# Which queue issues which transfer: 113 loads and stores leave the sync queue of a one-core decoder layer

## The chip, the core and the metric

One core of one Trainium2 chip runs the whole layer in one launch. The metric is device time in microseconds (us), median of three runs. Five engines work side by side, each on its own list of instructions, strictly in the order of that list: TensorE (PE in the profile, its weight loads PEld), VectorE (DVE), ScalarE (ACT), GpSimd (POOL) and SyncE (SP). SP computes nothing; it only issues transfers. A transfer is issued by one engine's list and waits there, at its place, until all it needs is ready; what stands behind it on that list waits too. Transfers that SP and ACT issue run on a hardware queue (q1 in the profile), those that POOL issues on a software queue (q0), and POOL's can also add to what lies in the destination (`accum_op=OP.add`).

## What is computed

```python
proj = x @ w_in[l]                       # 1024 tokens x 2048 -> one wide projection, split in 13
# group A: indexer scores, top-256 causal keys per query, latent attention, SiLU gate
score = einsum('bqh,bqhs->bqs', wb, relu(einsum('bqhd,bsd->bqhs', qib, k_idx)))
_, sel = top_k(where(causal, score, -inf), 256)
logits = einsum('bqhc,bqkc->bhqk', qb, ckv[sel]) * 128 ** -0.5 + rel_bias[t5_bucket(rel)]
o = einsum('bhqk,bqkc->bqhc', softmax(logits), ckv[sel])
y_a = einsum('bthc,hcd->bthd', o, w_uv[l]) * silu(z_a)
# group B: mLSTM, chunkwise, 4 heads, after a causal conv and SiLU on q and k; norm, two gates
y_m = norm(mlstm(q, k, v, i, f)) * sigmoid(o_m) * silu(z_m)
x = layer_norm(ALPHA * x + concat([y_a, y_m]) @ w_out[l])
```

## The kernel before

Every projection is a product of two float32 matrices with each operand split in a high and a low part, three matmuls a block (`xh,wh`, `xl,wh`, `xh,wl`). The blocks of 2 x 2 products are combined in Strassen's manner: seven products instead of eight, with summed weights (`t1` to `t4`) and summed inputs (`s1` to `s4`).

A weight block of 256 KB goes this way: SP loads it into one of six `wraw` buffers; for a sum, POOL adds a second block to it in flight (L722, L823), which has to wait until the first has landed; ACT rounds it to `wh` (L743, L850), DVE takes the rest as `wl` (L744, L851), and twelve matmuls of 512 columns use the pair. There are four buffers each for `wh` and `wl`.

The program runs in these stages (us from the start of the profile): narrow and query projections (0 to 230); 20 units of projections over the first half of the input, with the indexer's scores (240 to 690), each unit's partial result stored as 1 MB in `part_d` (L791); the value projections in two halves (`Values`, 690 to 845), with stores to `v_d` (L892) and loads of new input forms `u` (L284, L288); the second half of the units with the mLSTM of four heads (845 to 1292); attention (1292 to 1500); the output product with partial sums `z_d` (L1527) and the norm (to the end).

In the second half each unit first loads its partial result back (`res<-part_d`, L710), adds four products to it, and what the unit is for is done with it: a conv for q and k, a scaling and a store to `qa_d` (L974, L975), or a SiLU and a store to `gate_a` (L209, L210). Two `res` tiles take turns. Each half of a head loads gate rows broadcast to 128 partitions (`ri`, L994, then a POOL select L995), and its values (`vraw`, L1027), which ACT and DVE split (`vh`, `vl`) ahead of the state's matmuls (`num`, `up`).

The order on each engine is not that of the source: a scheduler simulates the program while it is built and puts each instruction on its engine's list where its simulation finds it ready; `urgent()` and the other priorities decide among those ready. So a change of a queue moves instructions on other engines too.

Of the kernel before, what the change touches and what calls it, by code (L numbers as in the profile page):

```python
# [30 lines left out]
DV = 256  # L31
# [14 lines left out]
G_QA = 16  # L46
# [56 lines left out]
def kernel(ctx, tc, a, out):  # L103
# [101 lines left out]
    def gate_attention(j, ps, z=None):  # L205
        z = s4("z") if z is None else z
        with urgent():
            for p_, s in zip(ps, halves):
                act.activation(z[:, s], p_, AF.Silu)  # L209
        sync.dma_start(gate_a[j], z)  # L210


    mi = [s4("mi", (P, min(3, 8 - 3 * i), NM)) for i in range(3)]
# [27 lines left out]
    for k in range(4):  # L241
        r, ws, xs = {}, [], []
# [227 lines left out]
    with tc.high_priority(offset=I_PRIO), tc.issue_after(marks[n + 46].ins):  # L470
        for j in range(2):
            cn = s4("cn")
            for h in range(2):
                ps = bank("cnt")
                for c in range(4):
                    pe.transpose(ps[:, c * P:(c + 1) * P],
                                 narrow(h * 4 + c, M_C + j * P, M_C + (j + 1) * P), ident)
                vec.tensor_scalar(cn[:, halves[h]], ps, small(S_KVG + j), None, op0=OP.mult)
            sync.dma_start(c_d[j], cn)
        gr = s4("gr", (2 * H_M, T))  # L480
        for h in range(2):
            ps = bank("gnt")
            for c in range(4):
                pe.transpose(ps[0:2 * H_M, c * P:(c + 1) * P], narrow(h * 4 + c, M_IF, NM), ident)
            act.copy(gr[:, halves[h]], ps[0:2 * H_M])
        sync.dma_start(if_d[:], gr)
# [136 lines left out]
    def search():  # L623

        yield from count(None, OP.is_ge)
        vec.tensor_scalar(sgn, cnt, TOPK - 0.5, -1.0, op0=OP.is_lt, op1=OP.mult)
        vec.memset(sel, 0)
        for bit in range(30, -1, -1):
            vec.scalar_tensor_tensor(out=cand, in0=sel, scalar=1 << bit, in1=sgn,  # L629
                                     op0=OP.bitwise_or, op1=OP.bitwise_xor)  # L630
            yield from count_both(cand.bitcast(F32))
            vec.tensor_tensor(take, cnt, bound, op=OP.is_le)
            vec.scalar_tensor_tensor(out=sel, in0=take, scalar=bit, in1=sel,
                                     op0=OP.logical_shift_left, op1=OP.bitwise_or)
        vec.tensor_tensor(thr.bitcast(I32), sel, sgn, op=OP.bitwise_xor)
        yield from count(thr, OP.is_gt)
        vec.tensor_scalar(take, cnt, TOPK - 0.5, None, op0=OP.is_ge)
        vec.tensor_scalar(low, sel, 0xffff, None, op0=OP.bitwise_and)
        vec.tensor_scalar(high, sel, 16, None, op0=OP.logical_shift_right)
        vec.tensor_tensor(low, low, take, op=OP.add)  # L640
        vec.tensor_scalar(take, low, 16, None, op0=OP.logical_shift_right)
        vec.tensor_tensor(high, high, take, op=OP.add)
        vec.tensor_scalar(low, low, 0xffff, None, op0=OP.bitwise_and)
        vec.scalar_tensor_tensor(out=sel, in0=high, scalar=16, in1=low,
                                 op0=OP.logical_shift_left, op1=OP.bitwise_or)
        vec.tensor_tensor(thr.bitcast(I32), sel, sgn, op=OP.bitwise_xor)
        yield from count(thr, OP.is_gt)
        vec.tensor_scalar(need, cnt, -1.0, float(TOPK), op0=OP.mult, op1=OP.add)
        for t in range(2, 8):
            w = (t + 1) * P  # L650
            col = slice(t - 2, t - 1)
            eq = s4("eq", (P, T), BF16)[:, 0:w]
            vec.tensor_scalar(eq, sc[t], thr[:, col], None, op0=OP.is_equal)
            yield
            pre = s4("pre")[:, 0:w]
            vec.tensor_tensor_scan(out=pre, data0=one_col[:, 0, 0:1].broadcast_to([P, w]), data1=eq, initial=0.0,
                                   op0=OP.mult, op1=OP.add)
            yield
            vec.scalar_tensor_tensor(out=pre, in0=pre, scalar=need[:, col], in1=eq,
                                     op0=OP.is_le, op1=OP.mult)  # L660
            yield
            vec.scalar_tensor_tensor(out=pre, in0=sc[t], scalar=thr[:, col], in1=pre,
                                     op0=OP.is_gt, op1=OP.max)
            yield
            m = s4("m", (P, T), BF16)[:, 0:w]
            vec.tensor_scalar(m, pre, -BIG, BIG, op0=OP.mult, op1=OP.add)
            sync.dma_start(mask_d[t][:], m)
            yield

    steps = search()  # L670
# [23 lines left out]
    class Unit:  # L694


        def __init__(self, i, g, second, X):
            self.i, self.g, self.second, self.X = i, g, second, X
            self.raw = {}
            if second and i == NU - 1:  # L700
                self.res = [s4("res") for _ in range(2)]
                with urgent():
                    for n in range(2):
                        sync.dma_start(self.res[n], part_d[i, :, n])
                return
            res = x_tile("res", (P, 2, T), F32)
            self.res = [res[:, n] for n in range(2)]
            if second:
                with urgent():
                    sync.dma_start(res, part_d[i])  # L710
            else:
                self.kept = res

# [73 lines left out]
        def end(self):  # L787
            self.product(self.pa, "t4", "a22", False)
            self.add(self.res[0][:, bot], self.pa, True)
            if not self.second:  # L790
                sync.dma_start(part_d[self.i], self.kept)  # L791

    heads = [[G_HEAD + 6 * h + 2 * j for j in range(3)] for h in range(H_M)]
    others = [G_QA + j for j in (0, 2, 4, 6)] + [G_ZA + j for j in (0, 2, 4, 6)]
# [19 lines left out]
    class Values:  # L814
# [11 lines left out]
        def run(self, second, X):  # L826
# [54 lines left out]
            def add(i, n, ps, first=False, minus=False, last=False):  # L881
                for t in range(4):
# [6 lines left out]
                        else:  # L889
                            act.copy(dst, ps[t])  # L890
                    if last and t % 2:
                        sync.dma_start(v_d[n, i, :, t - 1:t + 1], self.c[i, n][t // 2])  # L892

            pa = [pj() for _ in range(4)]
            block(0, 0)
# [71 lines left out]
    def other(g, r):  # L967

        for i in range(2):
            if g < G_QA:  # L970
                gate_attention(g - G_ZA + i, [r[i][:, s] for s in halves], r[i])
            else:
                with tc.high_priority(offset=I_PRIO):
                    act.mul(r[i], r[i], -DH ** -0.5)  # L974
                sync.dma_start(qa_d[g - G_QA + i], r[i])  # L975

    def y_sign(left, upper):

# [2 lines left out]
    def mlstm_store(h, j, hs, sg):  # L981
        for half in range(2):
            ps = bank("ht")
            for c in range(4):
                pe.transpose(ps[:, c * P:(c + 1) * P], hs[half][:, c, j * P:(j + 1) * P], ident)
            vec.scalar_tensor_tensor(out=sg[:, halves[half]], in0=ps, scalar=y_sign(h < 2, half == 0),
                                     in1=sg[:, halves[half]], op0=OP.mult, op1=OP.mult)
        sync.dma_start(y_d[8 + 2 * h + j], sg)

    def mlstm_half(h, half, n, q, k):  # L990

        s = halves[half]
        ri = s4("ri", (P, 2, 512))
        sync.dma_start(ri, bcast_rows(rows_d[h, :, s]))  # L994
        pool.affine_select(out=ri[:, 0].rearrange("p (c l) -> p c l", l=L),  # L995
                           in_=ri[:, 0].rearrange("p (c l) -> p c l", l=L),
                           compare_op=OP.is_ge, fill=BIG, base=0,
# [26 lines left out]

    def split_values(h, half):
        raw = s4("vraw", (P, 4, DV))
        sync.dma_start(raw, v_d[h // 2, half, :, :, h % 2 * DV:(h % 2 + 1) * DV])  # L1027
        vh, vl = s4("vh", (P, 4, DV + 2), F32R), s4("vl", (P, 4, DV + 2), F32R)
        split(vh[:, :, 0:DV], vl[:, :, 0:DV], raw)
        act.copy(vh[:, :, DV:DV + 2], one_col)  # L1030
# [401 lines left out]
    class Product:  # L1432
# [76 lines left out]
        def add(self, i, n, ps, first=False, minus=False, last=False):  # L1509
# [14 lines left out]
            if last and not self.c:  # L1524
                for t, z in enumerate(self.z[i, n]):
                    r0 = 4 * i + 2 * t
                    sync.dma_start(z_d[r0:r0 + 2, :, n].rearrange("t p c -> p t c"), z)  # L1527

        def run(self, then, following=None):
            pa = [lps() for _ in range(4)]  # L1530
# [143 lines left out]
```

## Time and profile before

| | |
|---|---|
| median of 3 runs | 1829.42 us (1828.87 to 1832.27) |
| the profiled execution | 1828.79 us, of which the span of the trace is 1827.0 us |
| TensorE busy | 1774.0 us, 97% of the span |
| VectorE, ScalarE, GpSimd busy | 1400.2, 943.5, 263.5 us |
| transfers | SP issues 794, GpSimd 192, ScalarE none |

The profiled execution lies within the range of the runs, 0.63 us under their median; 1.79 us of it lie outside the span. An engine's busy time leaves out the issuing of transfers and its waits. In the rows of the timeline the brackets give the engine's idle time ahead of an instruction and what ended it.

### The profile page before, as it was taken

To read this page: it belongs to the slowest core of one execution; us is meant where nothing else is said; L and a number is where in the kernel's file an instruction comes from. 1 tells how busy PE (TensorE), PEld (TensorE's weight loads), DVE (VectorE), ACT (ScalarE), POOL (GpSimd) and SP (SyncE) were. 2 spreads that over 40 slices of the span, in tenths; PEclk is the share of its full clock that TensorE was granted. 3 is DMA by queue.
4 is the path that set the end of the run, shared out by engine and by line. 5 is a ranking of instruction groups with operands and counts; after the bars stand their busy time and mean duration, and the time that the engine had idled before them with its cause. 6 is when DMAs were issued, how large, how long until landed. Compare 5 with 4: busy or idle time off the path is not lost. (4 is left out here: it accounts for less than half of the span.)

```text
span 1827.0 us, 25483 instructions
## 1 busy us (share of the span) xinstructions
PE 1774.0 (97%) x8613; PEld 1493.9 (82%) x8613; DVE 1400.2 (77%) x2674; ACT 943.5 (52%) x1728; POOL 263.5 (14%) x316
## 2 busy tenths in 40 slices
PE   8999999999999999999999999999989999999997
PEld 8788888887878888788888887878788987888885
DVE  8666677777877778887877786877898876676787
ACT  6343266566666658322555564565665654333410
POOL 3101110000100010100101000010454530011000
PEclk9999999999999999999999999999999999999998
DMA  9986254445575657887656656475776447965764
GB/s 329 324 296 196 84 166 120 111 127 136 136 207 143 167 166 240 291 251 199 204 174 180 198 149 181 108 202 176 236 202 159 118 115 216 279 191 123 188 190 139
DMA packets 148732, 338.82 MB, mean 185 GB/s; under 512 B 16104, under 2 KB 25576, under 8 KB 142456
## 3 DMA queue, kind: packets, MB, share of 16 engines
q1 hardware_dynamic: 121880, 280.16, 46.5%
q0 software_dynamic: 26720, 57.03, 16.5%
q8 instruction: 68, 1.11, 0.2%
q14 instruction: 64, 0.52, 0.1%
HBM read 259.40 MB, written 91.35 MB: 192 GB/s over the span
## 5 line engine op out<-in xcount | busy, mean ns | idle before, releaser
L753 PE MATMUL pj<-xh,wh 128*128 128x512 f32 x960 | 376.4, 393 | 5.9 <-DVE res L762 4.3
L753 PE MATMUL pj<-xl,wh 128*128 128x512 f32 x960 | 375.2, 391 | 0.0
L753 PE MATMUL pj<-xh,wl 128*128 128x512 f32 x960 | 371.2, 392 | 1.2 <-DVE wl L744 1.2
L743 ACT CAST wh<-wraw 128x512 fp32r<-128x512 f32 x280 | 172.2, 619 | 207.8 <-PE pj L753 92.3
L744 DVE TENSOR_TENSOR wl<-wraw,wh 128x512 fp32r<-128x512 f32 x280 | 191.3, 687 | 48.9 <-ACT wh L743 43.3
L753 PEld LDWEIGHTS pj<-xh,wh 128*128 128x128 f32 x960 | 180.6, 188 | 45.1 <-ACT pqh L108 3.0
L753 PEld LDWEIGHTS pj<-xh,wl 128*128 128x128 f32 x960 | 180.4, 188 | 38.1 <-DVE wl L744 2.3
L753 PEld LDWEIGHTS pj<-xl,wh 128*128 128x128 f32 x960 | 180.5, 188 | 34.5
L722 POOL DMA_DIRECT2D wraw<-wg x80 | 68.2, 856 | 753.3 <-DMA wraw<-wg 172.8
L762 DVE TENSOR_TENSOR res<-res,pj 128x512 f32<-128x512 f32 x160 | 109.2, 682 | 54.4 <-PE pj L753 44.9
L583 DVE SCALAR_TENSOR_TENSOR sc<-r,wi,sc 128x384 f32<-128x384 f32 (+2 forms) x90 | 84.1, 948 | 30.7 <-ACT r L578 30.0
L578 ACT ACTIVATE r<-sc 128x384 f32<-128x384 f32 (+3 forms) x160 | 79.2, 524 | 51.1 <-PE sc L577 37.3
L108 ACT CAST wh<-wraw 128x512 fp32r<-128x512 f32 (+2 forms) x88 | 50.2, 575 | 80.3 <-PE lps L1486 22.6
L614 ACT ACTIVATE junk<-sc,cand 128x512 bf16<-128x512 f32 (+2 forms) x93 | 86.7, 934 | 6.0 <-DVE cand L629 6.0
L109 DVE TENSOR_TENSOR wl<-wraw,wh 128x512 fp32r<-128x512 f32 (+2 forms) x88 | 56.7, 647 | 31.6 <-ACT wh L108 24.2
L617 DVE TENSOR_SCALAR_CACHE_REDUCE junk<-sc,cand 128x384 bf16<-128x384 f32 (+2 forms) x93 | 80.1, 875 | 0.9
L1318 POOL TENSOR_TENSOR nm<-mask,tb 128x256 f32<-128x256 bf16 (+3 forms) x64 | 66.6, 1119 | 83.5 <-DVE mn L1325 69.4
L753 PE MATMUL pb<-xh,wh 128*128 128x512 f32 x160 | 62.9, 393 | 0.0
L753 PE MATMUL pb<-xh,wl 128*128 128x512 f32 x160 | 62.5, 391 | 0.0
L753 PE MATMUL pb<-xl,wh 128*128 128x512 f32 x160 | 62.4, 390 | 0.0
L1330 ACT ACTIVATE lg<-lg,mn 128x256 f32<-128x256 f32 (+3 forms) x64 | 50.4, 790 | 15.8 <-DVE mn L1325 15.7
L341 PE MATMUL pj<-xh,wh 128*128 128x512 f32 x128 | 51.4, 402 | 4.5 <-ACT wh L108 4.5
(561 smaller groups left out, 4471.6 us busy)
## 6 DMA issues: line engine op xcount, KB each, us to landing
wraw<-wg SPq DMA_DIRECT2D x232, 256.0 KB, 4.1
wraw<-wg POOLq DMA_DIRECT2D x80, 256.0 KB, 5.2
part_d<-res SPq DMA_DIRECT2D x20, 1024.0 KB, 4.9
res<-part_d SPq DMA_DIRECT2D x19, 1024.0 KB, 8.5
wraw<-wo SPq DMA_DIRECT2D x64, 256.0 KB, 4.5
wraw<-wv SPq DMA_DIRECT2D x48, 256.0 KB, 5.9
v_d<-v SPq DMA_DIRECT2D x16, 512.0 KB, 5.3
z<-x SPq DMA_DIRECT2D x16, 512.0 KB, 4.2
```

What stands on the lines that cost most here:

```text
L109: vec.tensor_tensor(lo, src, hi.bitcast(F32), op=OP.subtract)
L341: last_mm[0] = pe.matmul(ps[u], w[:, k], x[:, k], start=start and k == 0 and n == 0, stop=k == 3 and n == 2, skip_group_check=True)
L578: act.activation(r[:, s], ps, AF.Relu)
L583: vec.scalar_tensor_tensor(out=sc[t], in0=r, scalar=wcol, in1=sc[t], op0=OP.mult, op1=OP.add)
L614: act.activation(junk, sc[t], AF.Sign, scale=-1.0, bias=th[:, t - 2:t - 1], accum_out=cnt[:, t - 2:t - 1])
L617: vec.tensor_scalar(junk, sc[t], th[:, t - 2:t - 1], 0.0, op0=OP.is_lt, op1=OP.add, accum_out=cnt[:, t - 2:t - 1])
L722: pool.dma_start(r, a["wg"][self.g + more[1], :, k0:k0 + 4, :], accum_op=OP.add)
L743: last_cast[0] = act.copy(wh, src)
L744: last_low[0] = vec.tensor_tensor(wl, src, wh.bitcast(F32), op=OP.subtract)
L753: last_mm[0] = pe.matmul(ps, w[:, k], x[:, k], start=start and k == 0 and n == 0, stop=k == 3 and n == 2, skip_group_check=True)
L762: vec.tensor_tensor(dst, dst, ps, op=OP.subtract if minus else OP.add)
L1318: last_sum[0] = pool.tensor_tensor(nm[:, 0:ws], mask[t][:, w - ws:w], tb[:, off:off + ws], op=OP.add)
```

## The change

The same transfers are made, in the same sizes, between the same tiles. 113 of SP's 794 are issued by another engine: 36 by ACT (the stores to `part_d`, `qa_d` and `gate_a`), 77 by POOL (2 to `c_d`, 6 to `mask_d`, 16 to `v_d`, 8 of `sg` to `y_d`, 8 to `z_d`; and 21 loads of `res`, 8 of `ri`, 8 of `vraw`). SP keeps the weights and the other loads.

```diff
@@ gate_attention (L210)
-        sync.dma_start(gate_a[j], z)
+        act.dma_start(gate_a[j], z)
@@ L479
-            sync.dma_start(c_d[j], cn)
+            pool.dma_start(c_d[j], cn)
@@ search (L667)
-            sync.dma_start(mask_d[t][:], m)
+            pool.dma_start(mask_d[t][:], m)
@@ Unit.__init__ (L704, L710)
-                        sync.dma_start(self.res[n], part_d[i, :, n])
+                        pool.dma_start(self.res[n], part_d[i, :, n])
...
-                    sync.dma_start(res, part_d[i])
+                    pool.dma_start(res, part_d[i])
@@ Unit.end (L791)
-                sync.dma_start(part_d[self.i], self.kept)
+                act.dma_start(part_d[self.i], self.kept)
@@ Values.run (L892)
-                        sync.dma_start(v_d[n, i, :, t - 1:t + 1], self.c[i, n][t // 2])
+                        pool.dma_start(v_d[n, i, :, t - 1:t + 1], self.c[i, n][t // 2])
@@ other (L975)
-                sync.dma_start(qa_d[g - G_QA + i], r[i])
+                act.dma_start(qa_d[g - G_QA + i], r[i])
@@ mlstm_store (L988)
-        sync.dma_start(y_d[8 + 2 * h + j], sg)
+        pool.dma_start(y_d[8 + 2 * h + j], sg)
@@ mlstm_half (L994)
-        sync.dma_start(ri, bcast_rows(rows_d[h, :, s]))
+        pool.dma_start(ri, bcast_rows(rows_d[h, :, s]))
@@ split_values (L1027)
-        sync.dma_start(raw, v_d[h // 2, half, :, :, h % 2 * DV:(h % 2 + 1) * DV])
+        pool.dma_start(raw, v_d[h // 2, half, :, :, h % 2 * DV:(h % 2 + 1) * DV])
@@ Product.add (L1527)
-                    sync.dma_start(z_d[r0:r0 + 2, :, n].rearrange("t p c -> p t c"), z)
+                    pool.dma_start(z_d[r0:r0 + 2, :, n].rearrange("t p c -> p t c"), z)
```

The engines' lists differ at three places that matter below. The first is on SP, in the value projections, around the loads of two input forms (`u_7111` and `u_7119`). Before:

```order
L821 DMA wraw_7253<-wv 128x512
L284 DMA u_7111<-form_d1s3_82 128x2048
L892 DMA v_d_75<-v_6489 128x1024
L892 DMA v_d_75<-v_6490 128x1024
L288 DMA u_7119<-xT 128x512 x4
```

In the changed kernel, on SP at the same place:

```order
L821 DMA wraw_7253<-wv 128x512
L284 DMA u_7111<-form_d1s3_82 128x2048
L288 DMA u_7119<-xT 128x512 x4
L879 DMA v_7143<-v_d_75 128x1024
```

The two stores between the loads are gone from SP. The second place is the mLSTM's third head, where its first half loads its values (`vraw_10173`). Before, on SP:

```order
L719 DMA wraw_10508<-wg 128x512
L710 DMA res_10279<-part_d_84 128x2048
L1027 DMA vraw_10173<-v_d_75 128x4x256
L719 DMA wraw_10531<-wg 128x512
```

In the changed kernel the same two loads stand on POOL, with a weight block's second part, which POOL adds to `wraw_10508`, between them:

```order
L722 DMA wraw_10451<-wg 128x512
L995 AFFINE_SELECT ri_10142<-ri_10142 128x512
L710 DMA res_10279<-part_d_84 128x2048
L722 DMA wraw_10508<-wg 128x512
L1027 DMA vraw_10173<-v_d_75 128x4x256
```

On ACT the cast of these values (`vh_10175`) stood before behind the weight casts `wh_10302` and `wh_10433`:

```order
L743 CAST wh_10302<-wraw_10202 128x512
L743 CAST wh_10433<-wraw_10431 128x512
L108 CAST vh_10175<-vraw_10173 128x4x256
L1031 ACTIVATE vl_10176<-one_col_68 128x4x2
L743 CAST wh_10454<-wraw_10451 128x512
L743 CAST wh_10474<-wraw_10451 128x512
```

In the changed kernel it stands behind two more weight casts and a sigmoid with its table load:

```order
L743 CAST wh_10433<-wraw_10431 128x512
L743 CAST wh_10454<-wraw_10451 128x512
L961 ACT_TABLE_LOAD
L961 ACTIVATE res_10065<-res_10065 128x1024
L743 CAST wh_10474<-wraw_10451 128x512
L108 CAST vh_10175<-vraw_10173 128x4x256
```

The third place is the fourth head, where POOL's list in the changed kernel puts the gate rows `ri_10983` and the partial result `res_11151` behind a weight block (`wraw_11380`) and two stores; before, SP had them ahead of the load of that same block:

```order
L722 DMA wraw_11323<-wg 128x512
L722 DMA wraw_11380<-wg 128x512
L988 DMA y_d_74<-sg_10321 128x1024
L988 DMA y_d_74<-sg_10570 128x1024
L994 DMA ri_10983<-rows_d_93 128x2x512
L710 DMA res_11151<-part_d_84 128x2048
L995 AFFINE_SELECT ri_10983<-ri_10983 128x512
```

So at this place a load that had the weights' queue to itself for a moment now waits for a weight block.

## Rows read from the trace of the kernel before

**Rows 1.** The page's first part: engine, busy us (share of the span), instructions.

```profile
PE 1774.0 (97%) x8613; PEld 1493.9 (82%) x8613; DVE 1400.2 (77%) x2674; ACT 943.5 (52%) x1728; POOL 263.5 (14%) x316
```

**Rows 2.** Windows: stretch, length, busy us of PE, PEld, DVE, ACT, POOL.

```profile
690.00:845.00 155.00, 150.97 (x661) 123.38 (x660) 135.81 (x233) 66.61 (x112) 12.01 (x14) 1.00 0.84 264
845.00:1292.00 447.00, 438.12 (x2110) 364.67 (x2109) 339.99 (x639) 254.76 (x412) 45.98 (x57) 1.00 0.61 173
...
200.00:250.00 50.00, 49.72 (x238) 40.98 (x238) 34.52 (x68) 22.63 (x54) 6.77 (x10) 1.00 0.42 135
```

**Rows 3.** Waits of the SP queue, whole span: us in total, times, longest.

```profile
SPq L719 <- DVE wraw L740: 279.9, 37, 14.5
...
SPq L479 <- DVE cn L478: 33.2, 1, 33.2
```

**Rows 4.** Waits of PE in the mLSTM's stage, 845 to 1292.

```profile
PE pj L753 <- DVE res L762: 4.3, 4, 2.6
PE num L112 <- ACT vh L108: 3.0, 2, 2.0
```

**Rows 5.** Timeline of SP, 744 to 770: start, us, what.

```profile
746.84 0.33 SPq L284 DMA_DIRECT2D u<-form_d1s  x1
748.62 1.51 SPq L892 DMA_DIRECT2D v_d<-v  x2
750.41 3.64 SPq L288 DMA_DIRECT2D u<-xT  x4
```

**Rows 6.** Timeline of ACT, 752 to 764.

```profile
757.88 1.05 ACT L108 CAST xh<-u 128x1024 fp32r<-128x1024 f32 x1 [3.49 <-DMA u<-xT]
```

**Rows 7.** Timeline of PE, 758 to 764.

```profile
759.99 0.50 PE L861 MATMUL pj<-wh,xh 128*128 128x512 f32 x1 [0.69 <-ACT v L890]
...
762.95 0.49 PE L861 MATMUL pj<-wh,xh 128*128 128x512 f32 x1 [1.75 <-ACT v L890]
```

**Rows 8.** Timeline of SP, 1098 to 1124.

```profile
1111.84 0.54 SPq L1027 DMA_DIRECT2D vraw<-v_d  x1
```

**Rows 9.** Timeline of POOL, 1105 to 1133.

```profile
1117.54 0.86 POOL L722 DMA_DIRECT2D wraw<-wg  x1 [9.38 <-DMA wraw<-wg]
```

**Rows 10.** Timeline of ACT, 1112 to 1123.

```profile
1120.94 1.05 ACT L108 CAST vh<-vraw 128x1024 fp32r<-128x1024 f32 x1 [5.86 <-DMA vraw<-v_d]
```

**Rows 11.** Timeline of PE, 1119 to 1123.

```profile
1122.05 0.39 PE L112 MATMUL num<-vh,pqh 128*128 128x258 f32 x1 [1.96 <-ACT vh L108]
```

**Rows 12.** Windows: the eleventh figure is the granted clock, 1.00 being full.

```profile
1123.50:1126.90 3.40, 3.40 (x13) 3.03 (x14) 3.22 (x6) 1.56 (x2) 0.00 (x0) 0.50 0.00 0
```

**Rows 13.** The tile vraw: issue to landing of its eight loads.

```profile
DMA to landing us min/median/max: 5.1/5.9/8.3
```

**Rows 14.** The chain that ended last, by time: start, us, what.

```profile
1607.64 10.88 PE lps L1486 x48
```

**Rows 15.** Transfer issues from 845 to 1292: KB each, median us to landing.

```profile
res<-part_d SPq DMA_DIRECT2D x17, 1024.0 KB, 8.5
```

**Rows 16.** Timeline of SP, 1198 to 1230.

```profile
1201.65 0.33 SPq L710 DMA_DIRECT2D res<-part_d  x1
```

**Rows 17.** Timeline of POOL, 1198 to 1230.

```profile
1209.73 0.86 POOL L722 DMA_DIRECT2D wraw<-wg  x1 [3.93 <-DMA wraw<-wg]
```

**Rows 18.** Timeline of DVE, 1215 to 1219.

```profile
1217.11 0.68 DVE L762 TENSOR_TENSOR res<-res,pj 128x512 f32<-128x512 f32 x1
```

**Rows 19.** The tile q_d, stored by SP and by POOL: ns min/median/max of an issue.

```profile
L370 SPq DMA_DIRECT2D q_d<-qres x8: 359/374/565, 57.9 to 131.9; - x8
...
L370 POOL DMA_DIRECT2D q_d<-qres x8: 707/713/762, 168.4 to 229.2; - x8
```

**Rows 20.** Transfer issues, whole span: those same stores, us to landing.

```profile
q_d<-qres SPq DMA_DIRECT2D x8, 512.0 KB, 5.2
...
q_d<-qres POOLq DMA_DIRECT2D x8, 512.0 KB, 3.1
```

**Rows 21.** Timeline of PE, 1526 to 1529.

```profile
1528.42 0.50 PE L1486 MATMUL lps<-wh,ys2h 128*128 128x512 f32 x1 [1.82 <-ACT wh L1424]
```

## The prediction

> **What bounds the kernel now.** I read the page's busy times first. TensorE is busy for 1774.0 of 1827.0 us [rows 1], so at most 53 us lie open to any change of queues, and much of that is the first load and the norm at the end, which the change does not touch. The reader is to see in the windows where the rest lies: TensorE is idle for 155.00 - 150.97 = 4.03 us in the value projections and 447.00 - 438.12 = 8.88 us in the mLSTM's stage [rows 2]. With the one wait in the output product that lies behind a load, 1.82 us [rows 21], and one stretch of 3.4 us at half clock behind a stall [rows 12], which costs 1.7 us, some 16.4 us are the most that the change could give back: 0.9%.
>
> Then I read what the sync queue waits for. Its largest entry is a weight that waits until DVE has read the buffer that it will fill, 279.9 us in 37 waits [rows 3]: SP is mostly early, and stands still because the weight buffers are full. The longest single wait for anything else is the store to `c_d`, 33.2 us, up to 230 us into the span, with weights behind it [rows 3]; in the window around its end TensorE was busy for 49.72 of 50 us [rows 2]. So a blocked SP by itself costs next to nothing; it costs where a load that some engine needs at once is late, and I looked for those in the timeline. There are two clear ones, in the values and in the third head.
>
> **The change, part by part.** The sum is made against the profiled execution, 1828.79 us: a span of 1827.0 us and 1.79 us around it; the median of the runs is 0.63 us above.
>
> *The values.* SP issued the input form `u_7111` at 746.84, then two stores that had to wait for DVE, then the next form's four loads from 750.41 on [rows 5]. Without the stores these can go from about 747.2 on, up to 3.2 us earlier. ACT waited 3.49 us for them and had its copies of `v` queued behind [rows 6], and TensorE waited for those copies, 0.69 and 1.75 us [rows 7]. The gain lies between nothing (DVE's own late pieces there end the same wait) and 2.44 us. I take 1.5, nearer to the upper end, since 3.2 us cover nearly all of the 3.49: **-1.5 us**.
>
> *The third head's values.* Before, `vraw_10173` was issued at 1111.84 [rows 8]; on POOL it stands behind the addition to `wraw_10508`, which was issued at 1117.54 for 0.86 us, since the block's first part had to land [rows 9]. Nothing in the change makes that part land earlier: SP had issued it ahead of both loads. So the load goes out at 1118.4, 6.6 us later, and with the median of 5.9 us [rows 13] it lands at 1124.3, 3.4 us after the 1120.94 at which ACT could begin [rows 10]. But the scheduler has put two weight casts ahead of it, which feed 24 matmuls; 48 take 10.88 us [rows 14], so TensorE has 5.4 us more to do first. 5.4 - 3.4 = 2.0 us covers the 1.96 us for which it waited there [rows 11], and if that stall goes, so does the half clock that follows it [rows 12]. The best case is 1.96 + 1.7 = 3.66 us gained, the worst 3.4 us lost, where ACT, held up by the late values, is late with the weights behind. I take a gain near the middle, since ACT still waits in order: **-1.0 us**.
>
> *The fourth head.* `res_11151` was issued at 1201.65 [rows 16]. On POOL it stands behind the addition to `wraw_11380`, issued at 1209.73 for 0.86 us [rows 17], two stores and the gate rows, each some 0.71 us on POOL [rows 19]: about 1212.7, or 11 us late, less what SP gains by not stopping for it. It took 8.5 us to land [rows 15], so before there were 1217.11 - 1210.2 = 7 us to spare until the first add [rows 18]. The loss is between nothing and 11 - 7 = 4 us; DVE has other work at this place, so I take the middle: **+2.0 us**.
>
> *The other loads on POOL.* 20 `res`, 8 `ri` and 6 `vraw` remain. On POOL's list they stand close to the time order they had, so most are late by an addition's wait or not at all. What TensorE waits for behind such loads in this stage is 4.3 + 3.0 us [rows 4], 5.3 without the stall counted above. Half of it could be won or as much be lost: -2.7 to +2.7; nothing speaks for a side, so **0**.
>
> *Issuing.* The 36 stores on ACT cost it about as much as on SP, 0.374 us each [rows 19], 13.5 us in all; they follow ACT's own results, so the wait is short. ACT is busy for 52% [rows 1]; hidden by its idle time, they cost what the share of TensorE's idle time is in the mLSTM's stage, 8.88 / 447 = 2% of 13.5: **+0.3 us**, 0 at best, 13.5 if nothing covered them. POOL's 77 issues take 77 x 0.713 = 55 us; it is busy for 14%, and what they hold up is priced above. The store to POOL's queue itself lands no later: 3.1 us there against 5.2 us by SP, in other stretches [rows 20]. So the landing is priced at nothing, the 48% of ACT's and 86% of POOL's time that is free being the cover.
>
> A rule speaks against the loads on POOL: the Trainium skill (DMA: Bandwidth & Descriptors, SWDGE vs HWDGE vs iDMA) says that GpSimd writes its descriptors in software into SBUF, where VectorE can lock it out, which SP's and ACT's queues never meet. By its first-byte figures (about 1 against 0.6 us, section Latency and other measured facts), my estimate is 0.4 us more for each of 37 moved loads, some 15 us of latency, of which most would be hidden; the rows on the stores show no such loss.
>
> *The output product.* The stall of 1.82 us [rows 21] comes from a form whose load stood behind a `z_d` store on SP, but which refills a buffer that DVE reads until the same moment. Gain between 0 and 1.82; I take **0**, as the buffer is the later one. *All that lies before 230 us* keeps its lists: **0**.
>
> Sum: -1.5 - 1.0 + 2.0 + 0 + 0.3 + 0 = -0.2, so 1828.6 us, 0.8 us under the median.
>
> **The rivals.** *Late loads vanish (faster).* SP, rid of stores, feeds the forms early and the new order covers the rest: 2.44 + 3.66 + 2.7 = 8.8 us less, 1820.0 us. For it: the first two stalls have a traced cause that the change removes. Against: loads of `res` were issued when their buffer came free, and no queue changes that.
>
> *GpSimd's queue becomes the one that blocks (slower).* The 38 additions in the mLSTM's stage each wait for a weight's first part, and loads now stand behind them. One such load that comes later than its cover costs what the one before did, 1.96 us and 1.7 us of half clock [rows 11, 12], 3.66 us. Two more than now cost 7.3 us: 1836.1 us. For it: 6.6 and 11 us at the two places above. Against: the scheduler moved casts behind. It decides from delays of about 5.4 us on, the cover of two weight blocks.
>
> *The queue is beside the point (no change).* All waits stay what they are because buffers, not queues, set the times: 1828.8 us. For it: the 33.2 us that cost nothing [rows 2, 3]. The Trainium skill (DMA: Bandwidth & Descriptors, Issuing engines are not separate DMA queues) says it as a rule: all transfers share the same engines, and issuing from several saves only the sequencers' time. By that rule, the sum without its first three terms would be +0.3 us; the trace agrees as far as that one wait goes.
>
> **How the numbers follow.** What a measurement of this kernel can tell from no change is 0.2%, 3.7 us: 1825.8 to 1833.1 us. My forecast, with gains and losses that nearly cancel, has 0.27, no change at all 0.14; nearly all of both lies within 0.2%, so same has 0.40. Late loads that vanish have 0.33, and a blocking GpSimd queue 0.26; I give faster 0.34 and slower 0.26. The likeliest one's own range is 1825.8 to 1833.1. To hold 8 in 10 the range has to reach to about the time of both other cases: 1820 to 1836 and a us beyond at either end, 1819 to 1837. The bounds of the terms (16.4 us of possible gain; 3.4 + 4 + 2.7 us of loss, and the issues) lie not far outside it.
>
> **What would show it.** Right: in the changed profile ACT's wait for `u<-xT` in the values is under 1 us and TensorE's waits for `v` are gone; ACT still waits several us for the third head's `vraw`, with no stall of TensorE near 2 us behind it; DVE waits for `res` in the fourth head; the idle time in the mLSTM's stage is between 6 and 12 us. It would be wrong if stalls of 2 us and more, each followed by a stretch at half clock, appeared where a load waits behind an addition on POOL; if the new order of the index products (240 to 690), which I price at nothing as TensorE hardly waits there, opened stalls; or if ACT, with stores in its list, were late with weight casts.

## The result, and the profile after

The changed kernel takes 1846.80 us (median of 6 runs), the kernel before 1829.89 us in the same runs: a ratio of 1.0093, with a 95% interval of 1.0076 to 1.0110. The forecast was 1828.6 us; the loss of 17 us lies outside its range. The profiled execution took 1849.4 us, with a span of 1847.6 us, 20.6 us longer than before. One execution of the last kernel of the experiments took 3595.72 us, about twice the rest, and its ratio leaves it out.

The page's busy times and its transfer queues (number and kind, packets, MB, share of 16 engines), changed kernel:

```profile
PE 1781.1 (96%) x8613; PEld 1493.5 (81%) x8613; DVE 1402.3 (76%) x2674; ACT 940.5 (51%) x1727; POOL 310.5 (17%) x393
...
q1 hardware_dynamic: 100488, 202.52, 34.4%
q0 software_dynamic: 37296, 105.30, 23.7%
q10 hardware_dynamic: 5184, 29.36, 4.0%
```

VectorE and ScalarE do the work of [rows 1]; TensorE is 7.1 us busier with the same 8613 matmuls, in part from more time at half clock. POOL's 47 us more are its 77 new issues: for GpSimd the page counts an issue as busy time, other than the text ahead of the prediction says. q10 is ScalarE's queue, which did not exist before; ScalarE's transfers do not run on q1.

Windows of the changed kernel, with columns as in [rows 2]: the index products, and the second units with the mLSTM.

```profile
230.00:484.00 254.00, 247.97 (x1114) 206.50 (x1114) 180.72 (x270) 151.92 (x307) 20.43 (x27) 0.99 0.46 124
855.00:1308.00 453.00, 437.35 (x2092) 360.92 (x2091) 337.76 (x636) 250.54 (x407) 67.29 (x95) 1.00 0.60 169
```

The same two stages of the kernel before are this window, and the second of [rows 2]:

```profile
230.00:475.00 245.00, 243.16 (x1109) 202.80 (x1107) 179.90 (x270) 152.70 (x306) 20.80 (x26) 1.00 0.48 128
```

TensorE's idle time grows from 1.84 to 6.03 us in the index stage and from 8.88 to 15.65 us in the mLSTM's. Behind the new stalls the clock falls to half, as it did behind the old one [rows 12]; two such stretches of the changed kernel:

```profile
916.40:919.80 3.40, 3.40 (x10) 2.63 (x9) 3.15 (x6) 3.15 (x6) 0.00 (x0) 0.50 0.39 141
438.50:445.30 6.80, 5.89 (x14) 4.01 (x15) 6.08 (x9) 3.53 (x8) 0.86 (x1) 0.50 0.26 44
```

The lag behind the kernel before, in these two traces, is 7.8 us when the last index product (L577) ends, 7.1 at the first and 12.0 at the last product of the values (L861), 21.1 at the last of the second units (L753), and no more after that. So the values lose about 5 us as well; their longest stall is followed by 3.4 us at half clock:

```profile
772.91 1.13 PE L861 MATMUL pj<-wl,xh 128*128 128x512 f32 x2 [2.76 <-DVE wl L851]
```

What TensorE waits for from 855 to 1308, changed kernel (us in total, times, longest); the longest entry was not in [rows 4]:

```profile
PE pb L753 <- DVE wl L744: 4.5, 2, 4.3
PE pj L753 <- DVE res L762: 3.9, 5, 1.7
PE num L112 <- ACT vh L108: 2.5, 3, 1.6
```

The timeline of the changed kernel at that wait:

```profile
903.49 0.86 POOL L722 DMA_DIRECT2D wraw<-wg  x1 [1.92 <-issue]
904.02 1.07 POOL L994 DMA_DIRECT2D ri<-rows_d  x1
...
914.20 1.15 DVE L1018 TENSOR_TENSOR pq<-q,ri 128x512 f32<-128x512 f32 x1 [7.71 <-DMA ri<-rows_d]
915.28 0.68 DVE L744 TENSOR_TENSOR wl<-wraw,wh 128x512 fp32r<-128x512 f32 x1
...
916.01 0.50 PE L753 MATMUL pb<-xh,wl 128*128 128x512 f32 x1 [4.34 <-DVE wl L744]
```

Read it upward. TensorE waits 4.34 us for the low part `wl` of a weight. VectorE had the weight, but stood in its row at `pq`, 7.71 us, for the gate rows `ri`. Their load went out 0.53 us behind an addition on GpSimd's queue, and landed 10.1 us later. In the kernel before SP issued the same load at 888.65; its landing is not in the trace, but the three of the eight whose landing is took 5.3 to 5.6 us. The half clock at 916.4 follows.

In the index stage, the changed kernel:

```profile
433.54 0.33 SPq L535 DMA_DIRECT2D hc<-max_d  x1
...
437.17 0.27 DVE L538 TENSOR_SCALAR gates<-gates,hc 32x128 f32<-32x128 f32 x1 [2.95 <-DMA hc<-max_d]
437.48 0.40 ACT L545 ACTIVATE gates<-gates,hc 32x128 f32<-32x128 f32 x1 [2.68 <-DVE gates L538]
...
438.39 0.59 PE L576 MATMUL sc<-khh,qb 128*128 128x384 f32 x1 [2.15 <-ACT r L578]
```

and the kernel before:

```profile
434.26 0.30 SPq L535 DMA_DIRECT2D hc<-max_d  x1
...
435.90 0.27 DVE L538 TENSOR_SCALAR gates<-gates,hc 32x128 f32<-32x128 f32 x1 [0.69 <-DMA hc<-max_d]
```

No transfer of this chain has changed its queue. What has changed is the order: the kernel before has two index reductions (L583) and two of ScalarE's rows (L578) ahead of the wait for the small load `hc` that the changed kernel has behind it, and the changed kernel stands and waits with TensorE behind it. The load was also slower here, 3.63 us from its issue to its reader instead of 1.64. This is one stall of a stage that lost 8 to 9 us; the run below that puts these rows back gains nothing by it.

### The profile page after: what moved, and what is told of

It reads as the page before. It is cut to its first block, busy times and chain, and to the rows that moved or that the text cites. A ratio compares the mean times of both kernels' runs of the same rounds, so it can differ in the third digit from the quotient of the medians.

```text
span 1847.6 us, 25493 instructions
## 1 busy us (share of the span) xinstructions
PE 1781.1 (96%) x8613; PEld 1493.5 (81%) x8613; DVE 1402.3 (76%) x2674; ACT 940.5 (51%) x1727; POOL 310.5 (17%) x393
## 4 chain that ended last, share of the span: by engine, by line
PE 70%; DMA 12%; DVE 9%; issue 5%; ACT 3%; POOL 1%; SPq 0%; DVEq 0%; POOLq 0%; ACTq 0%
PE pj L753 26%; PE lps L1486 6%; PE pb L753 5%; PE pj L861 4%; DMA wraw<-wg 3%; PE pj L341 2%; PE pc L861 2%; PE pc L1486 2%; PE sc L576 1%; PE sc L577 1%; DMA res<-part_d 1%; PE lps L112 1%; PE lps L113 1%; PE lps L114 1%; DMA vraw<-v_d 1%
## 5 line engine op out<-in xcount | busy, mean ns | idle before, releaser
L753 PE MATMUL pj<-xh,wh 128*128 128x512 f32 x960 | 377.3, 394 | 11.1 <-DVE res L762 4.3
L753 PE MATMUL pj<-xl,wh 128*128 128x512 f32 x960 | 375.6, 391 | 0.0
L753 PE MATMUL pj<-xh,wl 128*128 128x512 f32 x960 | 371.2, 392 | 0.5 <-DVE wl L744 0.4
L753 PEld LDWEIGHTS pj<-xh,wh 128*128 128x128 f32 x960 | 180.8, 188 | 52.0 <-ACT wh L743 8.2
L753 PEld LDWEIGHTS pj<-xh,wl 128*128 128x128 f32 x960 | 180.6, 188 | 39.1 <-DVE wl L744 2.8
L753 PEld LDWEIGHTS pj<-xl,wh 128*128 128x128 f32 x960 | 180.8, 188 | 35.4
L722 POOL DMA_DIRECT2D wraw<-wg x80 | 69.5, 869 | 693.0 <-DMA wraw<-wg 217.0
L583 DVE SCALAR_TENSOR_TENSOR sc<-r,wi,sc 128x384 f32<-128x384 f32 (+2 forms) x90 | 83.6, 948 | 27.1 <-ACT r L578 26.5
L578 ACT ACTIVATE r<-sc 128x384 f32<-128x384 f32 (+3 forms) x160 | 76.5, 524 | 43.6 <-PE sc L577 33.2
L753 PE MATMUL pb<-xh,wl 128*128 128x512 f32 x160 | 63.3, 396 | 4.5 <-DVE wl L744 4.5
L753 PE MATMUL pb<-xh,wh 128*128 128x512 f32 x160 | 63.7, 398 | 0.0
L753 PE MATMUL pb<-xl,wh 128*128 128x512 f32 x160 | 63.1, 395 | 0.0
L740 DVE TENSOR_TENSOR wraw<-wraw 128x512 f32<-128x512 f32 x80 | 55.4, 693 | 1.1
```

The lines of the kernel that those rows point to most:

```text
L578: act.activation(r[:, s], ps, AF.Relu)
L583: vec.scalar_tensor_tensor(out=sc[t], in0=r, scalar=wcol, in1=sc[t], op0=OP.mult, op1=OP.add)
L722: pool.dma_start(r, a["wg"][self.g + more[1], :, k0:k0 + 4, :], accum_op=OP.add)
L753: last_mm[0] = pe.matmul(ps, w[:, k], x[:, k], start=start and k == 0 and n == 0, stop=k == 3 and n == 2, skip_group_check=True)
```

## The experiments

Two things had changed together, the queues and the order that the scheduler wrote, so most runs hold one of them still. **Keeping an order.** In these kernels each engine's list is tied to that of another program, read from a table of places in the source's order. The ties order the issue and add no wait; a transfer that is on another engine than in the table is left out, and the scheduler places it. The ties themselves show no cost: three runs below whose lists are tied to the old order come out at 0.9994 to 0.9998.

```python
for engine, n in ISSUED:
    row = [traced[k] for k in place[start:start + n]]
    row = [i for i in row if i.engine == getattr(mybir.EngineType, engine)]
    for i, j in zip(row, row[1:]):
        tc.add_manual_dep(j, i.name, no_wait, reason="keep_order")
    start += n
```

"Old order" is that of the kernel before, "new order" that of the changed kernel. What the expectations call accumulations are the additions of L722. Every ratio below is to the kernel before in the same runs, and a loss in us is the ratio's part of 1829 us (17.0 for the changed kernel). Theory A was that the order makes the loss, theory B that the queues make it.

**New queues, old order; old queues, new order**

```diff
 # changed kernel with ORDER of the kernel before / kernel before with ORDER of the changed kernel
         tile_layer_kernel(ctx, tc, aps, out)
+        keep_order(nc, tc)
```

> All 113 transfers are on their new queues, but TensorE, VectorE, ScalarE and GpSimd run their instructions, and SP what is left to it, in the order of the kernel before; the scheduler places only the moved transfers. Theory A (the loss of about 17 us comes from the order that the scheduler writes anew from about 230 us on): about 1829 us, within 4 us of the kernel before, and the index products end near 473.5 us as before. Theory B (the loss comes from the queues themselves: loads that stand behind accumulations on GpSimd, stores in ScalarE's row): about 1847 us, as the changed kernel, with the losses in the values (5 us) and in the mLSTM stage (9 us) still there.

Measured: 1853.57 us, 1.0134 (1.0117 to 1.0150).

> The mirror of the run before: all transfers are on the queues of the kernel before, but every engine runs in the order that the scheduler wrote for the changed kernel. Theory A (order): about 1847 us, with the index products ending near 481 us. Theory B (queues): about 1829 us. If both parts matter, both runs lie between, and their losses should sum to about 17 us.

Measured: 1840.42 us, 1.0056 (1.0041 to 1.0071). Both parts cost, and they don't add: 24.5 us for the queues under the old order, 10.2 for the order on the old queues, 17.0 for both. The new order was written with the new queues in view, and they cost less in it (6.8 us). The traces part cleanly: from the first to the last matmul of L577 the index stage lasts 237.1 us before, 238.0 with new queues and old order, 246.7 with old queues and new order; the second units' stage loses 23 us in the first of these runs and none in the second.

**One group alone, the scheduler free**

```diff
-                sync.dma_start(part_d[self.i], self.kept)
+                act.dma_start(part_d[self.i], self.kept)
```

> Only the 20 stores of part_d move, from SP to ScalarE; the scheduler is free, and its order on TensorE differs from that of the kernel before from the first second unit on (about 230 us). Theory A (order): the index stage loses some 5 to 9 us although 20 issues of 0.33 us on ScalarE can't cost that, so 1834 to 1840 us. Theory B (queues): at most 20 x 0.33 = 6.6 us if every issue were paid in full, and near 0 as ScalarE has idle time there: 1829 to 1831 us.

Measured: 1836.47 us, 1.0047 (1.0030 to 1.0065), 8.6 us: as A has it.

```diff
-        sync.dma_start(ri, bcast_rows(rows_d[h, :, s]))
+        pool.dma_start(ri, bcast_rows(rows_d[h, :, s]))
 # likewise res (L704, L710) and vraw (L1027)
```

> Only the loads res, ri and vraw move, from SP to GpSimd; the order differs from that of the kernel before only from about 1000 us on. Theory B (queues): the late loads behind accumulations are here whole, so most of the 9 us that the mLSTM stage lost, 1836 to 1840 us. Theory A (order): whatever the new order of this stage happens to give, and the index and values stages as before; 1826 to 1838 us, and a wait of TensorE behind a load on GpSimd's queue is not the longest of the stage.

Measured: 1858.32 us, 1.0157 (1.0138 to 1.0175). The loads alone cost more than the whole change, and more than A or B expected.

**Which transfers: one group alone, old order.** The edits are the lines of the change for the group named, with `keep_order`; for `vraw`:

```diff
-        sync.dma_start(raw, v_d[h // 2, half, :, :, h % 2 * DV:(h % 2 + 1) * DV])
+        pool.dma_start(raw, v_d[h // 2, half, :, :, h % 2 * DV:(h % 2 + 1) * DV])
```

> The 21 loads of res alone go by GpSimd; the four computing engines keep the order of the kernel before. In the run with all queues moved under this order TensorE's wait for res grew from 4.3 to 7.2 us between 850 and 1310 us, so theory C (each load pays for itself, where it stands behind accumulations) gives +3 to +5 us, 1833 to 1835. Theory D (one cause for all: any load on GpSimd's queue delays the accumulations too, so the weights come late whichever load is moved) gives +10 us or more, and TensorE's longest waits are for wl.

Measured: 1835.07 us, 1.0032 (1.0021 to 1.0043).

> The 8 loads of ri alone go by GpSimd, old order. Theory C: this is the dearest of the three, since VectorE stands in its row at pq (wait 10.6 us before, 20.1 us with all queues moved) and the parts wl of the weights are queued behind it: +9 to +12 us, 1839 to 1842. Theory D: about as much as for res and vraw, each in proportion to its count (8 of 37), +4 to +6 us.

Measured: 1842.08 us, 1.0072 (1.0058 to 1.0086).

> The 8 loads of vraw alone go by GpSimd, old order. Theory C: TensorE's wait for vh grew from 3.0 to 5.5 us, so +2.5 to +5 us with the clock's loss, 1833 to 1835. Theory D: +4 to +6 us.

Measured: 1839.56 us, 1.0051 (1.0034 to 1.0067).

> All stores on their new queues (36 on ScalarE, 42 on GpSimd), the loads res, ri and vraw still on SP, old order. If the loads carry the loss of the queues (theories C and D), this is within 3 us of the kernel before, 1827 to 1833; if the stores carry a part of it, 1835 or more. The order that the scheduler wrote anew has no part in it.

Measured: 1828.00 us, 0.9998 (0.9987 to 1.0008). The 76 stores (40 of them on GpSimd, not 42) cost nothing. Each load pays for itself: 0.32, 0.72 and 0.51% for 21, 8 and 8 loads, so theory D, a price by count, falls; `res` and `ri` cost about a us more than C gave them, 5.9 and 13.2 us, and `vraw` twice as much, 9.3 us. Its run shows why. Timeline of the kernel with `vraw` alone moved:

```profile
930.34 0.84 POOL L722 DMA_DIRECT2D wraw<-wg  x1 [14.19 <-ACT vh L1030]
930.87 0.99 POOL L1027 DMA_DIRECT2D vraw<-v_d  x1
...
939.23 1.04 ACT L108 CAST vh<-vraw 128x1024 fp32r<-128x1024 f32 x1 [7.32 <-DMA vraw<-v_d]
...
940.33 0.39 PE L112 MATMUL num<-vh,pqh 128*128 128x258 f32 x1 [3.06 <-ACT vh L108]
```

and of the kernel before:

```profile
926.76 0.54 SPq L1027 DMA_DIRECT2D vraw<-v_d  x1
...
931.90 1.05 ACT L108 CAST vh<-vraw 128x1024 fp32r<-128x1024 f32 x1 [1.40 <-DMA vraw<-v_d]
```

The addition in front had idled GpSimd for 14.19 us; the load went out right behind it, 4.1 us later than before, of which 1.4 are the kernel's lag at this place, and took 8.4 us instead of 5.1. ScalarE's wait is 5.92 us longer, and TensorE, which had not waited here, waits 3.06.

**The loads one place earlier.** On GpSimd's list, the load changes places with the addition ahead of it (all 8 of `ri`; the 4 of `vraw` that stand behind one):

```diff
-L722 DMA wraw<-wg
 L994 DMA ri<-rows_d
+L722 DMA wraw<-wg
```

> As the run that moved ri alone (1842.1 us), but in GpSimd's row each of the 8 loads of ri now stands one place ahead of the accumulation behind which it stood (it was issued 0.54 us after it in all 8 cases). Theory E (the loads are late because they stand behind an accumulation that waits for its buffer, and then land behind its data): ri lands in about 5.3 us again and the run returns to 1829 to 1833 us. Theory F (GpSimd's queue is slow for such a load wherever it stands, or what it held back on SP now crowds it): 1838 us or more, and the landing stays at 7 us. If the accumulations pay instead, TensorE waits for wl or wh of the second units.

Measured: 1830.65 us, 0.9996 (0.9982 to 1.0009).

> As the run that moved vraw alone (1839.6 us), but the four of the eight loads that stood directly behind an accumulation on GpSimd's queue stand one place ahead of it; the other four stay behind the selection in ri, from which their buffer comes. If the place is the cause: TensorE's two gaps of 3.2 and 3.5 us at 937 and 1051 us, each behind such a load, go, the one of 3.4 us at 1121 us stays, and with the time at half clock behind the two the run gains 7 to 10 us, 1830 to 1833 us. If the queue itself is slow for these loads, or the accumulations pay: 1836 us or more.

Measured: 1827.74 us, 0.9994 (0.9984 to 1.0004). The loss of both loads is their place in the row. But the landing did not become shorter, as theory E had it. The tile `ri`, moved alone (first) and moved ahead (second), issue to landing:

```profile
DMA to landing us min/median/max: 5.7/7.1/9.4
```

```profile
DMA to landing us min/median/max: 7.4/7.9/12.1
```

The load is as slow as before, but early enough: it goes out 6 to 21 us earlier than in the run that moved `ri` alone (the lag of that run is in these figures), and VectorE's wait for it at `pq` between 845 and 1300 falls from 16.8 to 2.4 us, where the kernel before has 10.6. The landing does not refute E: moved ahead of one addition, six of the eight loads still go out within 0.6 us behind the addition before it, as here:

```profile
887.89 0.84 POOL L722 DMA_DIRECT2D wraw<-wg  x1 [15.35 <-DMA wraw<-wg]
888.43 1.06 POOL L994 DMA_DIRECT2D ri<-rows_d  x1
```

Over all kept traces the landing goes with what GpSimd issued just ahead. The loads of `vraw` with no transfer issued there in the 3 us before them landed after 4.5 us in the median (35 loads, 3.9 to 7.1), those within 1 us of another after 7.4 (39 loads, 5.2 to 11.1); for `ri` it is 3.9 to 4.2 us (6 loads, all in the fourth head) against 8.1 (70 loads, 5.4 to 12.1). No run changes the neighbour alone, so it is not shown as the cause.

**The loads on ScalarE's queue, old order**

```diff
-        pool.dma_start(ri, bcast_rows(rows_d[h, :, s]))
+        act.dma_start(ri, bcast_rows(rows_d[h, :, s]))
 # likewise res and vraw; all stores on SP
```

> The 37 loads res, ri and vraw alone move, and not to GpSimd but to ScalarE, whose queue carries nothing else; the four computing engines keep the order of the kernel before. Theory E (the accumulations ahead of them on GpSimd's queue make the loss): 1827 to 1834 us, with what ScalarE's issues cost. Theory G (the loss comes from leaving SP: the weight loads, no longer held up by these loads, run ahead and take the engines of the transfers): 1840 us or more, as on GpSimd. A load that waits for its buffer in ScalarE's row would show as ScalarE waiting at lines 994, 1027 or 710.

Measured: 1834.43 us, 1.0029 (1.0017 to 1.0041): just above E's range, and no G. The landing is about SP's, 5.0 us for `ri` (the median of three on record); what is lost is probably again a place in a row, with TensorE's longest wait 3.8 us for `vh`, but no run tests that.

**The order's part.** First one piece of the index stage, moved within the new order:

```diff
 L744 TENSOR_TENSOR wl<-wraw,wh
-L538, L539, L540, L551 (gates, hc)
 L583 SCALAR_TENSOR_TENSOR sc<-r,wi,sc
 L583 SCALAR_TENSOR_TENSOR sc<-r,wi,sc
+L538, L539, L540, L551 (gates, hc)
```

> The changed kernel in its own order, but for one piece at 437 us: the four VectorE rows of the gates (lines 538, 539, 540, 551), which wait for hc, stand behind the next two index reductions (line 583) and ScalarE's lines 545 and 541 behind the next two rows of line 578, as the kernel before has them. If the 9 us that the index stage lost are the order's, and this piece of it: TensorE's gaps of 2.15 and 0.53 us at 436 to 440 us go, and with them the 6.8 us at half clock behind them (3.4 us): 4 to 7 us less than the changed kernel, 1840 to 1843 us. If the piece is not the cause, 1846 to 1848 us.

Measured: 1847.52 us, 1.0095 (1.0079 to 1.0111). A miss: in its trace the index stage is 2.8 us shorter (243.7 instead of 246.5 us), the gap at 436 us being replaced by one of 1.6 us, but the kernel gains nothing that is measured.

> All stores on their new queues, the loads on SP, and the scheduler free to write its order. Under the old order this was 1828.0 us, so what it is above that is the price of the new order alone: theory A puts it at the 8 to 10 us that the index stage lost in every kernel whose order was written with part_d on ScalarE, 1836 to 1840 us. If the order's loss hangs on the loads' places too, within 3 us of the kernel before.

Measured: 1845.40 us, 1.0081 (1.0065 to 1.0098). The same queues cost nothing under the old order (0.9998), so with these queues the new order costs 14.8 us, more than expected.

The next two runs have tables put together from both orders:

```diff
 # all rows up to the last L577 from one order, the rest from the other
+row = [n for n in first[e] if n in early] + [n for n in second[e] if n not in early]
```

> The changed kernel with its queues; what comes before the last index product in the kernel before runs in that kernel's order, and all the rest in the order of the changed kernel. If the order's cost lies in the index stage alone: 9 us less than the changed kernel, 1836 to 1840 us, and what is left is the loads' in the second units. If it lies elsewhere, 1844 us or more.

Measured: 1845.87 us, 1.0090 (1.0075 to 1.0106).

> The mirror, on the queues of the kernel before: the index stage in the order of the changed kernel, the rest in the order of the kernel before. If the index stage carries the order's cost: 1836 to 1840 us, about what the whole new order cost on the old queues (1840.4 us). If not: within 3 us of the kernel before.

Measured: 1835.41 us, 1.0033 (1.0021 to 1.0045). The new order of the index stage costs 6.0 us in the kernel before; without it the changed kernel gains hardly anything. So something else keeps the changed kernel slow, and two more runs asked whether it is the loads. Both have the edit of the next section, in the changed kernel's own order and in that of the run with the old index stage.

> The changed kernel in its own order, with the loads put right: res back on SP, and 12 of the 16 loads of ri and vraw one place ahead of the accumulation that they stood behind (the other four have no accumulation ahead of them, or need what is). If the loads' place makes the queues' part of the loss here too, what is left is the order's: 1838 to 1842 us, as with the new order on the old queues (1840.4). If 1845 or more, the loads are not the cause in the changed kernel itself.

Measured: 1835.20 us, 1.0035 (1.0020 to 1.0050), less than expected.

> The same repair of the loads in the kernel whose index stage runs in the old order and whose rest in the new one (1845.9 us). If index order and loads together make the loss: 1829 to 1834 us. If the rest of the new order costs by itself, 1836 or more, and the difference from 1829 is its price.

Measured: 1833.84 us, 1.0027 (1.0014 to 1.0039). It is: with the loads put right, the changed kernel in its own order is rid of 10.6 of its 17.0 us. The 5 to 6 us left above the kernel before are not all that the order costs. With the same queues, `res` on SP and 12 loads ahead, the old order gives 0.9966 (the next section), so the new one is 0.69%, about 12.6 us, behind it. One trace of the repaired kernel shows both sides: it lies 9.1 us behind the kernel before at the last index product and 9.6 at the last product of the values, but only 3.4 at the last of the second units. What the old index stage brings to the repaired kernel is not settled, since the two intervals overlap.

**The change put right**

```diff
 # changed kernel, old order, res on SP; ri and vraw ahead of the additions on GpSimd's list
-                    pool.dma_start(res, part_d[i])
+                    sync.dma_start(res, part_d[i])
```

> The change put right: all stores on their new queues, ri and vraw on GpSimd one place ahead of the accumulations as in the two runs that move them alone, res left on SP, and the order of the kernel before for the four computing engines. From the parts (stores 1828.0, ri ahead 1830.7, vraw ahead as it comes out) no gain: 1826 to 1832 us. If the earlier loads take the waits away that TensorE has for vh and pq in the kernel before (3.0 us for vh between 845 and 1292 us, and 3.4 us of half clock behind them), up to 6 us faster, 1822 to 1825.

Measured: 1823.60 us, 0.9966 (0.9952 to 0.9979): faster than both kernels. All that TensorE waited for in its trace, 840 to 1285:

```profile
PE pj L753 <- DVE res L762: 4.0, 4, 1.6
PE num L112 <- ACT vh L108: 1.0, 1, 1.0
```

Of the two entries in [rows 4] the one for `vh` has gone from 3.0 to 1.0 us, and the stretch at half clock behind it [rows 12] is gone. Here these loads no longer stand behind SP's weights, and behind an earlier addition than in the changed kernel: the first `ri` goes out at 852.0 us instead of 864.0. That this makes the gain is not shown. With `vraw` alone moved ahead the wait for `vh` was as short,

```profile
PE num L112 <- ACT vh L108: 1.1, 1, 1.1
```

and neither that run nor `ri` ahead nor the stores alone were faster (0.9994, 0.9996, 0.9998). Why the three together gain 6.2 us stays open.

## Why the prediction was wrong

Two steps failed. The first is "The other loads on POOL", priced at 0 with 2.7 us to either side: "most are late by an addition's wait or not at all". The mechanism stood there, but as even odds, and bounded by what TensorE waited for before (5.3 us). A load that is made later can open stalls where there were none, so the waits of before are no bound on the loss. The runs put this term at +5.9 us for `res`, +13.2 for `ri` and +9.3 for `vraw` under the old order, and at 10.6 us in the changed kernel. The second is the new order, which the sum has at nothing ("the new order of the index products (240 to 690), which I price at nothing"): it cost 10.2 us on the old queues, 14.8 with the stores moved and about 12.6 with the loads put right.

- *Landing, priced at nothing* from the stores to `q_d` [rows 20]: wrong for `ri`, a store's row taken for a load. In the medians of single traces `ri` took 4.9 to 6.5 us by SP, 5.0 by ScalarE and 7.1 to 8.2 by GpSimd. The runs with the loads ahead show that this alone costs nothing. My estimate by the Trainium skill (DMA: Bandwidth & Descriptors, Latency and other measured facts) was 0.4 us more for a load. The trace agrees in the sign for `ri` (about 2 us) and not for `vraw` (6.5 us by either queue, in the median over all traces), and gives the loss to the place in the row instead.
- *The index stage, priced at nothing* since TensorE hardly waited there: wrong. That TensorE has no wait says that the order there is good, and a new one need not be: 6.0 us on the old queues, with the new order in this stage alone.
- *The values, -1.5:* the gain did not arise; the lower end, nothing, was right for the stores. In the run with the stores alone `u<-xT` held ScalarE for 1.9 us at most instead of 3.49 [rows 6], but its longest wait for the load ahead, `u<-form_d1s`, was 7.0 us instead of 4.9. Its waits for `u` were 18.6 us in all instead of 18.0, and TensorE's for ScalarE's copies of `v` 2.8 instead of 2.4. The changed kernel lost about 5 us in this stage, which the sum did not have.
- *The third head, -1.0:* right in direction. The load stands behind `wraw_10508` as foreseen, ScalarE waits 3.90 us for it instead of 5.86 [rows 10], TensorE 0.34 instead of 1.96 [rows 11], and no half clock follows: nearer to the best case than to 1.0. The load took 8.5 us to land; the 5.9 us of [rows 13] are the median of the four landings that the trace records, not of eight.
- *The fourth head, +2.0:* `res_11151` was issued at 1223.41, 21.8 us later than before [rows 16], most of it the kernel's own lag; VectorE waited 0.19 us for it. Mis-sized by 2 us.
- *Issuing, +0.3, and the stores:* right, 0.9998 for all 76. The Trainium skill (DMA: Bandwidth & Descriptors, Issuing engines are not separate DMA queues) says that transfers run on the same DMA engines whichever engine issues them, and that issuing from several saves only the time of the issue. The run agrees for these stores: the issuing engine does not matter.
- *The output product and all before 230 us, 0:* right; in the same run the wait of 33.2 us at `c_d` [rows 3] is gone from SP without a gain, and SP waits 34.5 us for a weight buffer instead.

Of the rivals it was the second that came, GpSimd's queue as the one that blocks, for the loads' part of the loss; the order's part was in none of them. Its price for a late load, 3.66 us, fits what `vraw` showed (a stall of 3.06 us, and half clock behind it). Its count of two was wrong, and so was its point: it asked for delays of 5.4 us, the cover of two weight blocks, where one of 5.9 us left TensorE waiting 3.06, so the cover was under 3.

What stays open: where in the new order its cost lies beyond the index stage, why orders written for other queues are 9 to 15 us longer than the old one (1836.5, 1840.4 and 1845.4 us, where the queues cost nothing or were the old ones), and why the change put right is faster than its parts. A profile shows one execution, and the runs of one kernel differ by some 8 us, those of the changed kernel by 14, so a stage's few microseconds are not to be read from one trace.

## What to carry to other kernels

Before moving a load to another queue, look at what it will stand behind there: an instruction in front that waits for something of its own holds the load for as long, and one place in the row was worth 10 to 14 us here. The 76 stores could go anywhere here, so measure the stores and the loads of such a change apart. And where a scheduler writes the order, compare a change with the order held still as well: here the order alone was worth 0.5 to 0.8%, and the whole change 0.9%.

## What the hardware showed

The 512 KB load of `ri`, broadcast to 128 partitions, took 1.05 us to issue on GpSimd against 0.41 on SP. By SP it landed after 4.1 to 8.9 us (28 landings on record over all runs, median 5.6), by GpSimd after 3.9 to 12.1 (80, median 7.9); `vraw` has a median of 6.5 us by both. Nor was GpSimd's queue always the slower: with nothing issued on it in the 3 us before, the same loads landed after 3.9 to 7.1 us, right behind another transfer after 5.2 to 12.1. I had not expected that moving `ri` ahead of the addition would leave the landing as long (7.9 us): it then stands behind the addition before, and only its start had to be earlier.
